# One decoder layer on one core: two more single matmuls in the stream, and the last 512 row columns in two banks

## The chip, the core and the metric

The kernel runs on one core of a Trainium2 chip. A core has TensorE (PE; loading its weights is shown apart, as PEld), VectorE (DVE), ScalarE (ACT), GpSimd (POOL) and SyncE (SP), which issues most of the transfers. TensorE reads from SBUF and writes to PSUM, whose banks hold 512 float32 numbers in each of 128 partitions. The metric is the device time of one execution in microseconds (us).

## The reference

One decoder layer on 256 prompt rows and 64 sample rows (8 × 8), all in float32, with shared weights:

```
xn = rms_norm(x, g_mix);  z = xn @ w_in            # B | C | h | q | k | v | gate_c | gate_a
y_conv = (B * conv3(C * h)) @ w_conv_out
y_attn = window_attention(q, k, v) @ w_attn_out     # window 128, bias, sinks
h = x + (sigmoid(gate_c) * y_conv + sigmoid(gate_a) * y_attn) @ w_o
hn = rms_norm(h, g_ffn)
h = h + (silu(hn @ w_gate) * (hn @ w_up)) @ w_down
y = rms_norm(h, g_final)
```

It returns y of the prompt and of the sample, the last keys and values, and the convolution states. The model width is 2048, the feed-forward width 5632.

## The kernel before

The 320 rows lie as columns: hT[p, k, t] holds feature 128 k + p of row t. Every weight tile is loaded once (`wraw`, on SP's queue) and split in two numbers of fewer bits, `whi` (ScalarE, line 129) and `wlo` (VectorE, line 130); the activations are split likewise (`xh`, `xl`). A product is then three matmuls of 320 columns for each 128 × 128 weights: hi by hi, hi by lo, lo by hi (`product`, line 176). All projections run so, one behind the other: k and v (`kv_product`), q, then four rounds of C, H and B, the gates, the outputs, the feed-forward layer.

Small work goes on beside them. The generator in `side_work` is advanced by one `yield` at each `tick`, that is behind each weight tile of a product. What it gives TensorE stands in the stream at that place. `first_norm` sums the squares over the partitions with two matmuls (`prb`, lines 199 and 200) and makes the row factors from it; `attention` makes the prompt's scores (`ps`, lines 549 and 552), the prompt's values (`prompt_pv`, `po`, line 611, matmuls of 64 and 32 rows or columns), and then the sample's attention (`pss`, line 716; `spo`, line 779). The PSUM tiles for it are handed out in turn from four banks (`ps_aux`).

`nudge` (line 195) is one matmul of 320 columns whose result nobody reads; its weights and columns are read as plain rows, not in the turned order of the products. There are three: in `kv_product`, behind the sample's scores, and behind the sample's values.

At the end the first 128 rows are wanted as rows. For columns 0 to 1535 that is done earlier. For the last 512 (from E0 = 1536), each k of the second half of w_down is a matmul with the activations as weights (`a_first(k)`, `a_low(k)`) and the 512 weight columns moving; they add up in one bank, `rowacc`, and the rest of h is added to it by four transposing matmuls with `ident` (line 1295). Then ScalarE squares the bank and sums it (`row_squares`, line 1162), a short chain on VectorE and ScalarE makes the factor r (lines 1309 to 1312), and the columns are scaled and sent (lines 1314 to 1325). Meanwhile VectorE scales the other 192 rows in seven pieces (line 1305), which SP sends.

Of the kernel before, what the change touches and what calls it, by code (L numbers as in the profile page):

```python
# [8 lines left out]
F32 = mybir.dt.float32  # L9
F32R = mybir.dt.float32r  # L10
AF = mybir.ActivationFunctionType
ALU = mybir.AluOpType
# [5 lines left out]
T = TP + NB * TS  # L18
# [9 lines left out]
P = 128  # L28
KC = D // P
# [9 lines left out]
E0 = D - 512  # L39
# [13 lines left out]
def hybrid_layer(ctx: ExitStack, tc: tile.TileContext, a: dict, o: list):  # L53
    nc = tc.nc
# [17 lines left out]
    def ps_aux(name):  # L72
        return aux[0].tile([P, 512], F32, tag="aux", name=name)
# [7 lines left out]
    def after(*marks):  # L81

        es = ExitStack()
        for m in marks:
            es.enter_context(tc.issue_after(m.ins))
        return es
# [56 lines left out]
    last = {}  # L143
# [49 lines left out]
    def nudge(rows, weights, n):  # L193
        x, w = (bass.AP(r.tensor, r.offset, [list(r.ap[0]), [1, m]]) for r, m in ((rows(0), n), (weights(0), P)))
        nc.tensor.matmul(ps_aux(u("nudge"))[:, :n], w, x, start=True, stop=True)
# [12 lines left out]
    ident = cst.tile([P, P], F32, name="ident")  # L208
# [50 lines left out]
    hT = xv[:, VW:VX].rearrange("p (k t) -> p k t", k=KC)  # L259
# [173 lines left out]
    def first_norm():  # L433

        squares(12, 13, 14, 15)
        nc.vector.tensor_scalar(nsink, sink_bc, -1.0, None, op0=ALU.mult)
        e_sb = pr.tile([P, 2, 2 * WIN], F32, tag="w", name="e_sb", bufs=1).rearrange("p g k -> p (g k)")[:NH, :EL]
        nc.vector.memset(e_sb, NEG)
        parts = two_rows(xacc, at_h(7), at_t[:, LEAD_A + 6 * at_row:LEAD_A + 6 * at_row + T])
        at, one_each = [_bucket(c) for c in range(WIN)], NBK // 2  # L440
        nc.gpsimd.tensor_copy(e_sb[:, WIN - 1:WIN - 1 + one_each], relT[:, :one_each])
        for b in range(one_each, NBK):
            c, n = WIN - 1 + at.index(b), at.count(b)
            nc.gpsimd.tensor_copy(e_sb[:, c:c + n], relT[:, b:b + 1].to_broadcast([NH, n]))
        yield
        prb = ps_aux("prb")
        over_partitions(prb[:, :T], parts)
        rstd_of(prb[:, :T], [P, T], "r1", spare, out=rb)
        nc.vector.tensor_scalar(rbq, rb, HD ** -0.5, None, op0=ALU.mult)
        for z in (vT, kT):  # L450
            for c in range(2):
                nc.vector.tensor_mul(z[:, c, :], z[:, c, :], rb)
        nc.vector.tensor_mul(rbsq, rb, rb)
        nc.gpsimd.dma_start(e_scr, e_sb)
        nc.gpsimd.dma_start(
            bias_s, bass.AP(e_scr.tensor, e_scr.offset + WIN - TS, [[EL, NH], [1, TS], [1, WIN + TS]])
        )
        for _ in range(3):
            yield

    yp = ExitStack()
    yy = yp.enter_context(tc.tile_pool(name="yy", bufs=1))
# [199 lines left out]
    def prompt_values(pv, scrs):  # L662
        sides = pv.tile([P, 2, WIN], F32, name="sides")
        nc.gpsimd.memset(sides, 1.0)
        nc.gpsimd.affine_select(
            out=sides[:, 0], in_=sides[:, 0], compare_op=ALU.is_ge, fill=0.0, base=-1, pattern=[[-1, WIN]],
            channel_multiplier=1,
        )
        nc.gpsimd.affine_select(
            out=sides[:, 0], in_=sides[:, 0], compare_op=ALU.is_ge, fill=0.0, base=B - 1, pattern=[[B, 4], [0, B]],  # L670
            channel_multiplier=-1,
        )
        nc.gpsimd.tensor_tensor(sides[:, 1], sides[:, 1], sides[:, 0], op=ALU.subtract)
        pts = [pv.tile([P, 2, 4, 4, B], F32, name=f"pT{kv}") for kv in range(NKV)]
        side = [pv.tile([P, 2, 2, 4, B], F32, name=f"side{kv}") for kv in range(NKV)]
        vm = [pv.tile([P, DKV], F32, name=f"vm{t}") for t in range(3)] + [vn[1]]
        mixes = ((0, 0, P, 0), (0, 0, B, 1), (1, 0, P, 0), (1, 0, 2 * B, 1), (2, 0, P, 1), (2, 3 * B, P, 0))
        for i in range(len(units) + 5):
            if i < len(units):
                kv, gp = units[i]  # L680
                nc.gpsimd.dma_start(pts[kv][:, gp].rearrange("p a n j -> p (a n j)"), scrs[i])
            if 2 <= i < 8:
                t, r0, r1, src = mixes[i - 2]
                nc.scalar.activation(vm[t][r0:r1], vn[src][r0:r1], AF.Copy)
            if i >= 5:
                kv, gp = units[i - 5]
                prompt_masked(sides, pts[kv][:, gp], side[kv][:, gp])
            yield
        prompt_pv(pts, side, vm)
        yield  # L690

    W2 = WIN + TS

# [417 lines left out]
    for half in range(2):  # L1111
# [41 lines left out]
        if half == 1:  # L1153
            ya = xp.tile([P, 2, D], F32, tag="xh", name="ya")
            y0, gfb = ya[:, 0, :], ya[:, 1, :]
            nc.gpsimd.dma_start(gfb, a["g_final"].partition_broadcast(P))
            ssf = op.tile([P, 4], F32, name="ssf")
            yacc = op.tile([P, TR], F32, name="yacc")

            def row_squares(i, src):  # L1160
                jk = op.tile([P, 512], F32, tag="jk", name=u("jk"))
                nc.scalar.activation(
                    jk[:, :src.shape[-1]], src, AF.Square, scale=D ** -0.5, accum_out=ssf[:, i:i + 1]
                )

            def rows_turn(c0):

                flipped = op.tile([P, 512], F32, tag="jk", name=u("yT")).rearrange("p (b k j) -> p b k j", b=4, k=4)
                nc.vector.transpose(
                    flipped.rearrange("p b k j -> p k b j"),  # L1170
                    hT[:, c0 // P:c0 // P + 4, 0:P].rearrange("p k (b i) -> p k b i", i=B),
                )
                rows = turned_rows(f"y_scr{c0}", flipped.rearrange("p b k j -> p (b k j)"), 4, 4 * B)
                nc.gpsimd.dma_start(y0[:, c0:c0 + 512], rows)

            def rows_of(c0):

                y = y0[:, c0:c0 + 512]
                nc.vector.tensor_add(y, y, ylow[:, c0:c0 + 512])
                row_squares(c0 // 512, y)  # L1180
                nc.vector.tensor_mul(y, y, gfb[:, c0:c0 + 512])

            def rest_square(k):
                sq = tmp("td", "sq")[:, :TR] if k else yacc
                nc.scalar.activation(sq, hT[:, k, P:T], AF.Square)
                return sq

            def rest_factor(k):
                rest = hT[:, k, P:T]
                last["hi"] = nc.scalar.activation(rest, rest, AF.Copy, scale=g_fin[:, k:k + 1])  # L1190

            def rest_of(chunks):

                for k in chunks:
                    sq = rest_square(k)
                    if k:
                        nc.vector.tensor_add(yacc, yacc, sq)
                    rest_factor(k)

            warm = op.tile([P, 1], F32, name="warm")  # L1200
            eps = op.tile([P, 1], F32, name="eps")
            nc.vector.memset(eps, EPS)
            with after(last["sig"]):
                nc.scalar.activation(warm, ones, AF.Abs_reciprocal_sqrt)
# [77 lines left out]
    for c in range(4):  # L1282
        rest_factor(E0 // P + c)

    for k in range(nf):
        (wh, wl), xhk, xlk = held[k], a_first(k), a_low(k)
        for m, x in enumerate((xhk, xlk)):
            last["mm"] = nc.tensor.matmul(rowacc, x, wh, start=k == m == 0, stop=k == nf - 1 and m == 1)
        if k == 3:
            with after(last["mm"]):  # L1290
                pn = ps_aux("pn")
                nc.tensor.matmul(pn[:, :TR], ones_r.bitcast(F32), yacc, start=True, stop=True)

                for c in range(4):
                    last["mm"] = nc.tensor.matmul(
                        rowacc[:, c * P:(c + 1) * P], hT[:, E0 // P + c, 0:P], ident, start=False, stop=False,
                        is_transpose=True,
                    )
    rf = sum_root(pn[:, :TR], [P, TR], "rn", op)
    yqs = [raw_tile().rearrange("p k n -> p (k n)")[:, :5 * TR].rearrange("p (k t) -> p k t", t=TR) for _ in range(4)]  # L1300
    ahead = ()
    for k0, k1 in ((0, 3), (3, 5), (5, 8), (8, 10), (10, 13), (13, 15), (15, KC)):
        yq = yqs[k0 // 5][:, k0 % 5:k0 % 5 + k1 - k0]
        with after(*ahead):
            ahead = (nc.vector.tensor_mul(yq, hT[:, k0:k1, P:T], rf.unsqueeze(1).to_broadcast([P, k1 - k0, TR])),)
        nc.sync.dma_start(y_r[:, k0:k1, :], yq)
    row_squares(3, rowacc)
    part = ssf[:, 3:4]
    nc.scalar.activation(r, part, AF.Abs_reciprocal_sqrt, bias=s3)
    nc.vector.scalar_tensor_tensor(v, part, -0.5, h3, op0=ALU.mult, op1=ALU.add)  # L1310
    nc.vector.scalar_tensor_tensor(v, r, r, v, op0=ALU.mult, op1=ALU.mult)
# [9 lines left out]
    act(1152, E0)  # L1321
    send(256, 768)
    nc.scalar.dma_start(y_0[:, 768:E0], y0[:, 768:E0])
    nc.vector.scalar_tensor_tensor(y0[:, es], rowacc, r, gfb[:, es], op0=ALU.mult, op1=ALU.mult)
    send(E0, D)


# [72 lines left out]
```

## Time and profile before

| | us |
|---|---|
| median of 3 runs | 1590.14 (1590.08 to 1590.64) |
| the profiled execution | 1589.86, of it the span from first to last instruction 1588.1 |
| TensorE busy | 1580.0 (99%) |
| VectorE, ScalarE, GpSimd busy | 881.6, 651.4, 128.5 |
| granted TensorE clock, mean | 0.999 |
| data moved | 266.09 MB, mean 168 GB/s |

In a row of the timeline stand the start, the duration, the engine, the line, the operation with output and inputs, the shapes and the count. Consecutive rows of one group are merged. Matmuls are pipelined, so their durations overlap; what one costs is the distance to the next start. In the view of groups, the numbers behind the bar are the time of the group in us, the mean of one in ns, and the idle time before them.

### The profile page before, as it was taken

The page shows a single profiled execution, that of the slowest core. Times are in us where ns is not written, and L with a number is a line of the kernel's source. Part 1 is how long each engine was busy: PE and PEld are TensorE (multiplying, and loading weights), DVE is VectorE, ACT ScalarE, POOL GpSimd, SP SyncE. Part 2 cuts the span into 40 slices and gives each one's busy share as a digit, 9 for nine tenths or more (in the row PEclk, how much of TensorE's full clock was granted, in tenths as well). Part 3 has the DMA queues.
Part 4 walks back from the last instruction along what each step waited for, and adds up shares of the span by engine and source line. Part 5 has one row for each costly group of instructions (what it writes and reads, how often), then busy time and mean ns, then how long its engine had stood idle before and what let it go on. Part 6 is the DMA issues. An engine that isn't in the chain of part 4 may idle for free.

```text
span 1588.1 us, 27217 instructions
## 1 busy us (share of the span) xinstructions
PE 1580.0 (99%) x11315; PEld 1566.3 (99%) x11315; DVE 881.6 (56%) x1263; ACT 651.4 (41%) x913; POOL 128.5 (8%) x228
## 2 busy tenths in 40 slices
PE   9999999999999999999999999999999999999998
PEld 9999999999999999999999999999999999999887
DVE  7888765544455445565555555553443455555556
ACT  7554444333333334344333333333333333344443
POOL 2223242000000003320000000000000000000000
PEclk9999999999999999999999999999999999999999
DMA  8666666454444544444444445455555544544653
GB/s 276 204 191 193 213 205 207 160 157 157 152 158 159 159 158 153 156 158 160 157 153 156 158 159 159 154 154 158 159 159 156 155 157 158 160 159 152 186 191 122
DMA packets 77714, 266.09 MB, mean 168 GB/s; under 512 B 9816, under 2 KB 13240, under 8 KB 77464
## 3 DMA queue, kind: packets, MB, share of 16 engines
q1 hardware_dynamic: 71880, 249.86, 49.7%
q0 software_dynamic: 5280, 13.82, 2.9%
q8 instruction: 88, 1.44, 0.4%
q10 hardware_dynamic: 432, 0.69, 0.1%
q14 instruction: 34, 0.28, 0.1%
HBM read 257.25 MB, written 9.04 MB: 168 GB/s over the span
## 4 chain that ended last, share of the span: by engine, by line
PE 99%; DVE 0%; ACT 0%; DVEq 0%; issue 0%
PE fu L176 19%; PE fg L176 19%; PE dn L1059 12%; PE wo L176 7%; PE ga L176 7%; PE gc L176 7%; PE B L176 3%; PE H L176 3%; PE C L176 3%; PE q L176 3%; PE ya L176 3%; PE yc L176 3%; PE dn L1084 3%; PE kv L372 2%; PE dn L1092 2%; PE dl L1088 1%
## 5 line engine op out<-in xcount | busy, mean ns | idle before, releaser
L130 DVE TENSOR_TENSOR wlo<-wraw,whi 128x1024 fp32r<-128x1024 f32 (+1 forms) x460 | 560.9, 1220 | 574.3 <-ACT whi L129 563.4
L129 ACT ACTIVATE whi<-wraw 128x1024 fp32r<-128x1024 f32 (+1 forms) x460 | 485.0, 1056 | 699.5 <-PE fu L176 131.5
L176 PE MATMUL fu<-hh_t,whi 128*128 128x320 f32 x704 | 205.0, 301 | 0.0
L176 PE MATMUL fu<-hl_t,whi 128*128 128x320 f32 x704 | 205.0, 301 | 0.0
L176 PE MATMUL fg<-hh_t,whi 128*128 128x320 f32 x704 | 205.0, 301 | 0.0
L176 PE MATMUL fg<-hl_t,whi 128*128 128x320 f32 x704 | 205.0, 301 | 0.0
L1059 PE MATMUL dn<-a_t,whi 128*128 128x320 f32 x896 | 162.6, 301 | 0.0
L176 PE MATMUL fg<-hh_t,wlo 128*128 128x320 f32 x704 | 158.8, 301 | 0.0
L176 PE MATMUL fu<-hh_t,wlo 128*128 128x320 f32 x704 | 158.8, 301 | 0.0
L1059 PEld LDWEIGHTS dn<-a_t,whi 128*128 128x128 f32 x896 | 137.5, 187 | 0.0
L176 PEld LDWEIGHTS fu<-hh_t,whi 128*128 128x128 f32 x704 | 131.7, 187 | 0.0
L176 PEld LDWEIGHTS fu<-hl_t,whi 128*128 128x128 f32 x704 | 131.6, 187 | 0.0
L176 PEld LDWEIGHTS fg<-hh_t,whi 128*128 128x128 f32 x704 | 131.6, 187 | 0.0
L176 PEld LDWEIGHTS fg<-hl_t,whi 128*128 128x128 f32 x704 | 131.6, 187 | 0.0
L176 PEld LDWEIGHTS fg<-hh_t,wlo 128*128 128x128 f32 x704 | 116.1, 187 | 0.0
L176 PEld LDWEIGHTS fu<-hh_t,wlo 128*128 128x128 f32 x704 | 116.1, 187 | 0.0
L1059 PE MATMUL dn<-a_t,wlo 128*128 128x320 f32 x448 | 103.9, 301 | 0.0
L1059 PEld LDWEIGHTS dn<-a_t,wlo 128*128 128x128 f32 x448 | 74.8, 187 | 0.0
L176 PE MATMUL gc<-xh_t,whi 128*128 128x320 f32 x256 | 74.5, 301 | 0.0
L176 PE MATMUL gc<-xl_t,whi 128*128 128x320 f32 x256 | 74.5, 301 | 0.0
L176 PE MATMUL ga<-xh_t,whi 128*128 128x320 f32 x256 | 74.5, 301 | 0.0
L176 PE MATMUL ga<-xl_t,whi 128*128 128x320 f32 x256 | 74.5, 301 | 0.0
(328 smaller groups left out, 2801.9 us busy)
## 6 DMA issues: line engine op xcount, KB each, us to landing
wraw<-in_w_in_dram SPq DMA_DIRECT2D x128, 512.0 KB, 3.7
wraw<-in_w_gate_dram SPq DMA_DIRECT2D x88, 512.0 KB, 3.6
wraw<-in_w_up_dram SPq DMA_DIRECT2D x88, 512.0 KB, 3.6
wraw<-in_w_down_dram SPq DMA_DIRECT2D x88, 512.0 KB, 3.6
wraw<-in_w_o_dram SPq DMA_DIRECT2D x32, 512.0 KB, 3.6
wraw<-in_w_conv_out_dram SPq DMA_DIRECT2D x16, 512.0 KB, 3.7
wraw<-in_w_attn_out_dram SPq DMA_DIRECT2D x16, 512.0 KB, 3.8
wraw<-in_w_kv_dram SPq DMA_DIRECT2D x6, 512.0 KB, 7.6
```

The costliest lines, as they stand in the source:

```text
L129: last["hi"] = nc.scalar.activation(hi, src, AF.Copy)
L130: last["lo"] = nc.vector.tensor_sub(lo, src, hi.bitcast(F32))
L176: last["mm"] = nc.tensor.matmul(turns(fives(ps[c][:, :T])), w[:, k, c * P:(c + 1) * P], turns(x(kc)), start=(kc == 0 and i == 0), stop=(kc ...
L372: last["mm"] = nc.tensor.matmul(turns(fives(ps[c][:, :T])), w[:, k, c * P:(c + 1) * P], turns(x(kc)), start=(kc == 0 and m == 0), stop=(kc ...
L1059: last["mm"] = nc.tensor.matmul(turns(fives(ps[c][:, :T])), parts[k][w][:, c * P:(c + 1) * P], turns(x(k)), start=k == 0 and m == 0, stop= ...
L1084: nc.tensor.matmul(turns(placed(ps[c])), parts[k][0][:, cs], turns(a_move(k)), start=k == 0, stop=False)
L1088: nc.tensor.matmul(low, a_low(k), parts[k][0], start=k == 0, stop=k == nf - 1)
L1092: last["mm"] = nc.tensor.matmul(turns(placed(ps[c])[:, :, 0:JT]), parts[k][1][:, cs], turns(a_move(k)[:, :, 0:JT]), start=False, stop=k == ...
```

## The change

It does three things. `first_norm` issues a nudge one step behind its two sums. `prompt_values` issues one a step behind `prompt_pv`. And the last 512 row columns are summed in two banks of 256 columns, `rowacc` and `rowacc2`: for all k but the last four, left and right in turn; for the last four, first all of the left, then all of the right. The left bank is squared by itself, its sum goes into s3 and h3 ahead of the last scaled piece of the other rows, and the last scaling is done half by half.

```
-        for _ in range(3):
-            yield
+        yield
+        nudge(xh, xl, T)
+        yield
+        yield
...
         prompt_pv(pts, side, vm)
         yield
+        nudge(xh, xl, T)
...
-    for k in range(nf):
+    halves = [rowacc, ps_aux("rowacc2")]
+    order = [(k, h) for k in range(nf - 4) for h in range(2)] + [(k, h) for h in range(2) for k in range(nf - 4, nf)]
+    for k, h in order:
         (wh, wl), xhk, xlk = held[k], a_first(k), a_low(k)
         for m, x in enumerate((xhk, xlk)):
-            last["mm"] = nc.tensor.matmul(rowacc, x, wh, start=k == m == 0, stop=k == nf - 1 and m == 1)
-        if k == 3:
+            last["mm"] = nc.tensor.matmul(
+                halves[h][:, :256], x, wh[:, h * 256:(h + 1) * 256], start=k == m == 0, stop=k == nf - 1 and m == 1
+            )
+        if (k, h) == (3, 1):
...
-                        rowacc[:, c * P:(c + 1) * P], hT[:, E0 // P + c, 0:P], ident, start=False, stop=False,
-                        is_transpose=True,
+                        halves[c // 2][:, c % 2 * P:(c % 2 + 1) * P], hT[:, E0 // P + c, 0:P], ident, start=False,
+                        stop=False, is_transpose=True,
...
+        if k1 == KC:
+            row_squares(3, halves[0][:, :256])
+            with after(*ahead):
+                nc.vector.tensor_add(s3, s3, ssf[:, 3:4])
+                ahead = (nc.vector.tensor_scalar(h3, s3, -0.5, None, op0=ALU.mult),)
...
-    row_squares(3, rowacc)
-    part = ssf[:, 3:4]
+    row_squares(4, halves[1][:, :256])
+    part = ssf[:, 4:5]
...
-    nc.vector.scalar_tensor_tensor(y0[:, es], rowacc, r, gfb[:, es], op0=ALU.mult, op1=ALU.mult)
+    for h in range(2):
+        cs = slice(E0 + h * 256, E0 + (h + 1) * 256)
+        nc.vector.scalar_tensor_tensor(y0[:, cs], halves[h][:, :256], r, gfb[:, cs], op0=ALU.mult, op1=ALU.mult)
```

Where the nudges land is set by the ticks. TensorE's order behind the first norm's sums, at the end of a weight tile of the first q product, before (`q` are the product's two banks, `whi` and `wlo` the weight parts; left out are two more of wlo):

```order
L176 MATMUL q_497<-xh_t,whi_614 128x16x5x4
L176 MATMUL q_497<-xl_t,whi_614 128x16x5x4
L176 MATMUL q_496<-xh_t,wlo_615 128x16x5x4
L176 MATMUL q_497<-xh_t,wlo_615 128x16x5x4
...
L176 MATMUL q_496<-xh_t,whi_644 128x16x5x4
L176 MATMUL q_496<-xl_t,whi_644 128x16x5x4
```

And with the change:

```order
L176 MATMUL q_497<-xh_t,whi_614 128x16x5x4
L176 MATMUL q_497<-xl_t,whi_614 128x16x5x4
L176 MATMUL q_496<-xh_t,wlo_615 128x16x5x4
L176 MATMUL q_497<-xh_t,wlo_615 128x16x5x4
...
L195 MATMUL nudge_642<-xh_t,xl_t 128x320
L176 MATMUL q_496<-xh_t,whi_646 128x16x5x4
```

The nudge stands between two weight tiles, 24 matmuls behind the sums; the rest of the order is as it was.

TensorE behind the prompt's values, where the last H product of a round ends and B begins, with the semaphores that are waited for, before and then with the change:

```order
L176 MATMUL H_2455<-xh_t,whi_2612 128x16x5x4
L176 MATMUL H_2455<-xl_t,whi_2612 128x16x5x4
L176 MATMUL H_2455<-xh_t,wlo_2613 128x16x5x4 x4
L176 MATMUL B_2676<-xh_t,whi_2680 128x16x5x4 [waits Activation_49]
L176 MATMUL B_2676<-xl_t,whi_2680 128x16x5x4
```

```order
L176 MATMUL H_2457<-xh_t,whi_2614 128x16x5x4
L176 MATMUL H_2457<-xl_t,whi_2614 128x16x5x4
L176 MATMUL H_2457<-xh_t,wlo_2615 128x16x5x4 x4
L195 MATMUL nudge_2642<-xh_t,xl_t 128x320 [waits DVE_49,PE_49]
L176 MATMUL B_2680<-xh_t,whi_2684 128x16x5x4 [waits Activation_49]
```

The nudge takes the first of the four banks of `po`, so it waits for VectorE, which empties them.

VectorE at the end, from the pieces of the other rows (`wraw` are their buffers) on, before and then with the change (`s` and `h` are s3 and h3, `vf` and `rr` the factor r, `ya` holds the rows):

```order
L1305 TENSOR_TENSOR wraw_16162<-xv,rnr 128x384
L1305 TENSOR_TENSOR wraw_16163<-xv,rnr 128x192
L1310 SCALAR_TENSOR_TENSOR vf<-ssf,h_16078 128x1
...
L1314 TENSOR_SCALAR ya<-ya,rr 128x512
L1324 SCALAR_TENSOR_TENSOR ya<-rowacc,rr,ya 128x512
```

```order
L1317 TENSOR_TENSOR wraw_16199<-xv,rnr 128x384
L1314 TENSOR_TENSOR s_16081<-s_16081,ssf 128x1
L1315 TENSOR_SCALAR h_16082<-s_16081 128x1
L1317 TENSOR_TENSOR wraw_16200<-xv,rnr 128x192
L1322 SCALAR_TENSOR_TENSOR vf<-ssf,h_16082 128x1
...
L1326 TENSOR_SCALAR ya<-ya,rr 128x512
L1338 SCALAR_TENSOR_TENSOR ya<-rowacc,rr,ya 128x256
L1338 SCALAR_TENSOR_TENSOR ya<-rowacc_16116,rr,ya 128x256
```

Two operations of one column now stand ahead of the last piece, and the last scaling is two operations.

More of the change, by code (lines that the diff above doesn't have):

```diff
@@ L1156, in hybrid_layer @@
             nc.gpsimd.dma_start(gfb, a["g_final"].partition_broadcast(P))
-            ssf = op.tile([P, 4], F32, name="ssf")
+            ssf = op.tile([P, 5], F32, name="ssf")
             yacc = op.tile([P, TR], F32, name="yacc")
```

## The prediction

> **What bounds the kernel now.** I read the page first, its busy times and the chain that ended last.
>
> ```profile
> span 1588.1 us, 27217 instructions
> PE 1580.0 (99%) x11315; PEld 1566.3 (99%) x11315; DVE 881.6 (56%) x1263; ACT 651.4 (41%) x913; POOL 128.5 (8%) x228
> PE 99%; DVE 0%; ACT 0%; DVEq 0%; issue 0%
> ```
>
> TensorE is the bound from end to end: 99% of the chain is matmuls. An inserted matmul therefore costs its place in the stream in full, nothing hides it, and whatever changes the pace of the stream counts once per matmul. The other engines matter only behind the last matmul. So I went to the timeline of TensorE, where the distance from start to start is what one matmul costs (the durations of 0.30 overlap). First an ordinary stretch, then the one behind the prompt's values, and the windows view of both:
>
> ```profile
> 230.30 0.30 PE L176 MATMUL C<-xl_t,whi 128*128 128x320 f32 x1
> ...
> 240.10 0.30 PE L176 MATMUL H<-xl_t,whi 128*128 128x320 f32 x1
> ```
>
> ```profile
> 204.12 0.30 PE L176 MATMUL B<-xh_t,whi 128*128 128x320 f32 x1
> ...
> 213.79 0.73 PE L176 MATMUL B<-xh_t,wlo 128*128 128x320 f32 x4
> ...
> 215.58 0.41 PE L176 MATMUL B<-xh_t,whi 128*128 128x320 f32 x1
> ...
> 219.09 0.31 PE L195 MATMUL nudge<-xh_t,xl_t 128*128 128x320 f32 x1
> 219.24 0.30 PE L176 MATMUL C<-xh_t,whi 128*128 128x320 f32 x1
> 219.38 0.30 PE L176 MATMUL C<-xl_t,whi 128*128 128x320 f32 x1
> ```
>
> ```profile
> 204.30:214.30 10.00, 10.00 (x72) 9.96 (x71) 6.50 (x9) 4.69 (x9) 9.59 (x21) 1.00 0.87 287
> 230.30:240.30 10.00, 10.00 (x74) 10.00 (x73) 4.33 (x5) 3.19 (x3) 4.04 (x8) 1.00 0.92 296
> ```
>
> In the ordinary stretch 70 matmuls start between the two rows: 9.80 / 70 = 0.1400 us each, and I find the same nearly everywhere. From 204.12 to 213.79 there are 68: 9.67 / 68 = 0.1422 each. The same shapes run 2.2 ns slower, at the same granted clock (1.00 in both windows) and without idle time. The slow pace begins behind the prompt's values (which end at 200.6), outlasts the sample's scores (214.45 to 215.58), and ends at the nudge of 219.09: from there it is 0.14 again. That is what a nudge does in this trace. It is worth 2.2 ns for each matmul up to the next thing that would have restored the pace anyway.
>
> **The nudge behind the first norm's sums** (one more matmul on TensorE, first row at 42.71 in the time of before). It costs what a nudge costs in an ordinary stretch, and saves what the stretch behind it loses now.
>
> ```profile
> 15.36 0.31 PE L195 MATMUL nudge<-xh_t,xl_t 128*128 128x320 f32 x1
> ...
> 16.52 0.30 PE L372 MATMUL kv<-xl_t,whi 128*128 128x320 f32 x1
> ```
>
> ```profile
> 39.06 0.30 PE L199 MATMUL prb<-at_t,ones_r 128*128 128x320 f32 x1
> 39.20 0.31 PE L200 MATMUL prb<-at_t,ones_r 128*128 128x320 f32 x1
> ...
> 39.77 0.30 PE L176 MATMUL q<-xl_t,whi 128*128 128x320 f32 x1
> ...
> 42.71 0.30 PE L176 MATMUL q<-xh_t,whi 128*128 128x320 f32 x1
> ```
>
> The nudge of 15.36 and seven ordinary matmuls took 1.16 us; seven take 0.98, so it cost 0.18 (its own 0.147 and some ns at each of the next few). Behind the norm's sums 21 matmuls start between 39.77 and 42.71: 2.94 / 21 = 0.140. The pace there is the good one already, so in this execution there is nothing to restore: **+0.18**. Lower end: not below −0.56, the rival below; upper end +0.18, unless the nudge harms the pace (another rival). No engine waits for it, and its bank is one that nobody has still to read.
>
> **The nudge behind the prompt's values**, ahead of the first B matmul, 204.12. By the row of 219.09 a nudge in a slow stretch costs 0.29 for itself and one matmul, 0.15 more than that matmul at 0.14. Behind it stand 72 slow matmuls up to the sample's scores (68 and the last four): 72 × 2.2 ns = 0.16 saved. If the scores do not bring the slow pace back, the 24 between 215.58 and 219.09 save 0.05 more. I take both: 0.15 − 0.21 = **−0.06**; ends −0.06 and, if nothing is cured, +0.18. This nudge also adds a wait, since its bank is the first of the four that the prompt's values filled. Who empties it:
>
> ```profile
> 201.09 2.74 DVE L643 TENSOR_TENSOR at_t<-po,at_t 128x256 fp32r<-128x256 f32 x8 [2.88 <-ACT at_t L642]
> ```
>
> The last of these eight ends at 203.83, 0.29 before TensorE comes to the nudge. Even if it waited for all eight it would not stand; and what is queued behind it, the B product, would be late by no more than the overrun.
>
> **The tail.** Before, the last 512 columns are 32 matmuls of 512 columns; now 64 of 256, with the weights loaded twice as often.
>
> ```profile
> 1572.47 2.02 PE L1288 MATMUL rowacc<-a_t 128*128 128x512 f32 x8
> 1574.32 0.53 PE L1292 MATMUL pn<-yacc,ones_r 128*128 128x192 f32 x2
> ...
> 1575.04 1.17 PE L1288 MATMUL rowacc<-a_t 128*128 128x512 f32 x4
> 1576.05 2.02 PE L1288 MATMUL rowacc<-more,a_t 128*128 128x512 f32 x8
> 1577.91 2.91 PE L1288 MATMUL rowacc<-whi,a_t 128*128 128x512 f32 x12
> ```
>
> ```profile
> 89.75 0.40 PE L549 MATMUL ps<-k,at_t 128*128 128x256 f32 x2
> ...
> 90.46 0.31 PE L176 MATMUL C<-xh_t,whi 128*128 128x320 f32 x1
> ```
>
> ```profile
> L1288 PE MATMUL rowacc<-whi,a_t 128*128 128x512 f32 x12 | 2.9, 391 | 0.0
> L549 PE MATMUL ps<-k,at_t 128*128 128x256 f32 x32 | 6.0, 279 | 0.0
> ```
>
> 512 columns cost (1577.91 − 1576.05) / 8 = 0.232. The nearest rows for 256 are the prompt's scores: six of 256 columns, each with its weights, from 89.75 to 90.46, 0.118. So the first 16 take 1.89 instead of 1.85, +0.04. The other 48 begin with the same pause behind the transposes (1576.05 − 1575.04 is 0.08 over 4 × 0.232); their last start is 1575.04 + 0.08 + 47 × 0.118 + 0.04 = 1580.71. Now the last ends at 1580.82 (row of 1577.91), and a 256 ends 0.279 behind its start: 1580.99, **+0.17**. A rule weighed here: the Trainium skill ("TensorE: Matmul & The Clock Gate", section "Back-to-back issue gap") gives N / 2.4 + 2.5 ns from matmul to matmul; that would be 109.2 ns for 256 columns and 215.8 for 512, a split of only +0.08 over 64 against 32, where the rows make +0.13; as an estimate by that page the tail would be 0.05 better. The rows of this trace lie above the rule in both sizes (118 and 232), so I go by the rows.
>
> Ends of this pitch: half of a 512, 0.116, and the 0.140 of a 320-column matmul, the next wider shape. That is −0.13 and +1.39 over 63 pitches; I take 0.118, the row of the same width.
>
> Behind the last matmul (the waits of ScalarE, VectorE and the last sends):
>
> ```profile
> 1580.86 0.60 ACT L1162 ACTIVATE jk<-rowacc 128x512 f32<-128x512 f32 x1 [5.24 <-PE rowacc L1288]
> 1581.35 0.19 ACT L1162 ACTIVATION_READ_ACCUMULATOR jk<-rowacc 128x1 f32 x1
> ...
> 1582.36 0.75 DVE L1314 TENSOR_SCALAR ya<-ya,rr 128x256 f32<-128x256 f32 x2
> 1582.74 1.39 SPq L1316 DMA_DIRECT2D out_dram<-ya  x3
> 1583.02 0.75 DVE L1324 SCALAR_TENSOR_TENSOR ya<-rowacc,rr,ya 128x512 f32<-128x512 f32 x1
> ```
>
> ```profile
> L1185 ACT ACTIVATE sq<-xv 128x192 f32<-128x192 f32 x15 | 5.3, 359 | 12.3 <-DVE xv L1270 5.5 <-DVE yacc L1197 3.6 <-DVE xv L1105 3.2
> ...
> L1181 DVE TENSOR_TENSOR ya<-ya 128x512 f32<-128x512 f32 x3 | 2.1, 691 | 1.3 <-ACT jk L1162 1.3
> ```
>
> ```profile
> L851 DVE TENSOR_TENSOR qt<-q,rbq 128x256 f32<-128x256 f32 x8 | 3.4, 420 | 0.1
> ```
>
> ```profile
> 1580.69 0.36 DVE L1305 TENSOR_TENSOR wraw<-xv,rnr 128x192 f32<-128x192 f32 x1
> ```
>
> The left half's squares now run while TensorE makes the right half: eight matmuls, 8 × 0.118 = 0.94, cover one ACTIVATE and its read of the sum. What stays on the path is a Square of 256 instead of 512. Between 192 columns (359 ns) and 512 (0.60) a column costs 0.75 ns, so **−0.19**. The added sum and h3 on VectorE (two operations of one column, about 0.16 each) stand ahead of the last quotient of the other rows. The left sum is there at 1580.99 − 0.94 + 0.04 + 0.41 + 0.19 = about 1580.7, when that quotient started until now (1580.69); it and its send go about 0.35 later, and the send is not among the last, which begin at 1582.74: 0. The last scaling becomes two of 256. VectorE does 256 in 420 ns and 512 in 691, so a half costs about 0.75 − 0.27 = 0.48, and with the overlap of the pair at 1582.36 two take 0.87: **+0.12**. That is not covered, since the last send waits for the right part. Tail: 0.17 − 0.19 + 0.12 = **+0.10**, ends −0.15 (the low pitch, the scaling's extra covered by the transfers ahead of it) and +1.5 (the high pitch).
>
> **The sum** is 0.18 − 0.06 + 0.10 = +0.22. The profiled execution took 1589.86 (span 1588.1 and 1.8 around it) and would take 1590.1; the median of the runs, 1590.14, lies 0.28 above it, and on it I forecast 1590.3 to 1590.4. A change of under 0.2% (3.2 us) is about what a measurement here cannot tell from none; this one is a fifteenth of that.
>
> **Rivals.** (a) *A slow stretch that the profiled execution did not have.* The median is 0.28 over it, and the slow pace is there in one stretch, so the norm's sums may leave it in other executions. Up to the first prompt's scores (89.75) 336 matmuls × 2.2 ns = 0.74; the first nudge would gain 0.56 instead of losing 0.18. Against it: the only trace shows 0.140 there. Time 1589.6. (b) *The small matmuls do not reach 0.118 in the tail*, since their weights change at every instruction and come from tiles that are read as rows: at 0.140 the tail is +1.5 and the time 1591.7. For it: 512 columns cost 0.232 here. (c) *The change harms the pace, the other side.* The pace is a state that a few odd matmuls set and that nothing ordinary clears. If the new nudge of 42.71 leaves the slow one, it lasts to the prompt's values, 1104 matmuls, 2.4 us: 1592.7, still inside 0.2%. If the shifted sequence leaves it slow behind the last nudge at 254.9, the 8600 matmuls up to 1460 lose 18.9 us: 1609. It decides from about 1450 slow matmuls (3.2 us) on. Against it: the three nudges of before all end in 0.140. (d) *The change does nothing for the pace:* the second nudge leaves 0.1422; +0.18 instead of −0.06, 1590.6, inside the main range.
>
> **How the numbers follow.** Main case, (d) included, 0.76, time 1590.3, its own range 1589.9 to 1591.0 (the runs of before already spread from 1590.08 to 1590.64). (a) 0.10, (b) 0.07, (c) 0.04 for the short and 0.015 for the long form; 0.015 for what I do not see, split over both signs. A range from 1589.5 to 1591.2 holds the main case and (a), 0.86 less some noise. Faster by over 0.2% would need 1450 matmuls that run slow now, and I find 96: 0.01. Slower by over 0.2%: the long form of (c) and half of the unseen, 0.025. The rest, 0.965, is no change.
>
> **What would show it.** A nudge at about 42.7 with 0.18 lost around it; a nudge at 204.3, and 0.140 instead of 0.1422 behind it up to the sample's scores; 64 matmuls in the tail at 0.118, the left Square about 0.9 ahead of the right one, a right Square of about 0.41. I would be wrong if a long stretch reads 0.142, if TensorE shows a gap at the second nudge, or if the tail's pitch is near 0.14.

## The result, and the profile after

The changed kernel took 1602.43 us (median of 22 runs, 1590.03 to 1603.39), the kernel before 1590.24 in 22 runs beside them (1589.63 to 1603.14). The ratio is 1.0061, with a 95% interval of 1.0047 to 1.0075: slower by 0.6%, where I had forecast no change (the ratio takes in the runs of both groups named below; the two medians lie 12.2 us apart, 0.8%). A single execution of either kernel falls near 1590 or near 1602, with nothing between. Of the changed kernel's runs 19 of 22 were near 1602, of the runs before 3 of 22. The profiled executions were one of each majority: 1602.66 after, 1589.86 before.

The page of the changed kernel, its span, its busy times and the shares of the chain that ended last:

```profile
span 1601.0 us, 27294 instructions
PE 1592.9 (99%) x11349; PEld 1580.8 (99%) x11349; DVE 883.1 (55%) x1266; ACT 652.0 (41%) x915; POOL 128.2 (8%) x228
PE 99%; DVE 0%; ACT 0%; issue 0%; DVEq 0%
```

TensorE is still the bound, and 34 more matmuls cannot be 12.9 us. So the pace had changed somewhere, and the windows view finds where. Its columns are the stretch, its length, then busy time and instructions of PE, PEld, DVE, ACT and POOL, the granted clock, the DMA share and GB/s. First before, then after:

```profile
206.00:213.00 7.00, 7.00 (x51) 7.00 (x51) 5.23 (x7) 2.70 (x4) 6.99 (x12) 1.00 0.90 277
256.00:700.00 444.00, 444.00 (x3174) 444.00 (x3173) 227.13 (x269) 173.41 (x202) 35.60 (x34) 1.00 0.50 159
720.00:1400.00 680.00, 680.00 (x4860) 680.00 (x4859) 335.74 (x410) 250.12 (x295) 0.00 (x0) 1.00 0.51 157
```

```profile
206.00:213.00 7.00, 7.00 (x52) 7.00 (x51) 4.88 (x7) 3.31 (x5) 6.99 (x13) 1.00 0.94 304
256.00:700.00 444.00, 444.00 (x3173) 444.00 (x3172) 226.57 (x269) 174.44 (x205) 36.47 (x36) 1.00 0.49 159
720.00:1400.00 680.00, 680.00 (x4783) 680.00 (x4783) 331.19 (x402) 246.57 (x287) 0.00 (x0) 1.00 0.49 155
```

From 256 to 700 the two are alike. From 720 to 1400 TensorE is busy without a gap in both, at a granted clock of 1.00 in both, but does 4783 matmuls instead of 4860: 142.2 ns each against 139.9 (those cut at the edges counted). Where that begins is in the timeline of TensorE, after:

```profile
705.32 0.73 PE L176 MATMUL fg<-hh_t,wlo 128*128 128x320 f32 x4
705.89 0.31 PE L199 MATMUL pss<-a_t,ones_r 128*128 128x320 f32 x1
706.03 0.31 PE L200 MATMUL pss<-a_t,ones_r 128*128 128x320 f32 x1
706.18 0.30 PE L176 MATMUL fu<-hh_t,whi 128*128 128x320 f32 x1
...
707.17 0.30 PE L176 MATMUL fu<-hl_t,whi 128*128 128x320 f32 x1
```

Here stand the sums of the *second* norm (`pss`, lines 199 and 200: the same helper as for the first norm), which the change does not touch. The seven matmuls from 706.18 to 707.17 take 0.99, about 0.142 each. The same place before, six matmuls from 705.58 to 706.42 in 0.84, 0.140 each:

```profile
705.29 0.30 PE L199 MATMUL pss<-a_t,ones_r 128*128 128x320 f32 x1
705.43 0.31 PE L200 MATMUL pss<-a_t,ones_r 128*128 128x320 f32 x1
705.58 0.30 PE L176 MATMUL fu<-hh_t,whi 128*128 128x320 f32 x1
...
706.42 0.30 PE L176 MATMUL fu<-hh_t,whi 128*128 128x320 f32 x1
```

The pace stays so. Behind these sums stand 5472 product matmuls up to the second half of w_down; they take 778.24 us after (706.18 to 1484.42) and 766.08 before (705.58 to 1471.66), 142.22 and 140.00 ns each. That is 12.2 of the 12.9 us. About 0.4 more is lost at the start, where it varies from execution to execution: there the first products step by 267 ns, up to 6.46 us instead of 5.66, and the profile's record of the granted clock begins at 6.56 instead of 5.74. Over the profiles of before, after and the experiments this record begins anywhere from 3.5 to 6.6. So the first nudge stands at 43.15, where its place was forecast from 42.71. About 0.3 is the sum of the three local terms.

**Two streams of 140 ns.** Why do the same sums leave 140.00 before and 142.22 after, when what runs into them has a pace of 140 in both? The groups by line, from 300 to 690, in both kernels (mean ns of one behind the comma), before and then after:

```profile
L176 PE MATMUL gc<-xh_t,whi 128*128 128x320 f32 x224 | 65.2, 301 | 0.0
```

```profile
L176 PE MATMUL gc<-xh_t,whi 128*128 128x320 f32 x224 | 65.3, 302 | 0.0
```

A matmul lasts 301 ns before and 302 after, and not as a mean alone: shortest, median and longest of the 224 are all 301, or all 302. The step, from start to start, is 140 in both, so the span does not show it. The ends of matmuls are modelled in these profiles, so I take the 1 ns as a mark that tells two streams apart, and not as work. The weight loads of these `gc` rows carry it too: 187 ns shortest, median and longest before, 187, 188 and 188 after. I call them kind 301 and kind 302. Both kinds occur in the kernel before itself, which has this row from 222 to 245, behind its second nudge:

```profile
L176 PE MATMUL H<-xh_t,whi 128*128 128x320 f32 x31 | 9.1, 302 | 0.0
```

After, the same stretch has the other kind:

```profile
L176 PE MATMUL H<-xh_t,whi 128*128 128x320 f32 x28 | 8.2, 301 | 0.0
```

With that the chain can be followed, stretch by stretch (odd I call a matmul that belongs to no ordinary product: the nudges, the sums, the attention's). Before: the prompt's values leave the slow pace (durations of 303 to 305), the sample's scores keep it, the nudge of 219.09 turns it into kind 302, the sample's values turn kind 302 into 301, the last nudge, 254.88, and the second norm's sums leave 301 as it is. After, the timeline of TensorE:

```profile
204.73 0.31 PE L195 MATMUL nudge<-xh_t,xl_t 128*128 128x320 f32 x1
204.88 0.30 PE L176 MATMUL B<-xh_t,whi 128*128 128x320 f32 x1
205.02 0.30 PE L176 MATMUL B<-xl_t,whi 128*128 128x320 f32 x1
...
219.66 0.31 PE L195 MATMUL nudge<-xh_t,xl_t 128*128 128x320 f32 x1
...
252.37 0.30 PE L176 MATMUL B<-xh_t,whi 128*128 128x320 f32 x1
...
254.93 0.73 PE L176 MATMUL B<-xh_t,wlo 128*128 128x320 f32 x4
255.50 0.31 PE L195 MATMUL nudge<-xh_t,xl_t 128*128 128x320 f32 x1
255.64 0.30 PE L176 MATMUL B<-xh_t,whi 128*128 128x320 f32 x1
```

The new nudge at 204.73 turns the slow pace into kind 301; the scores and the nudge of 219.66 leave 301. The sample's values turn 301 into the slow pace: from 252.37 to 254.93 there are 18 matmuls, 2.56 / 18 = 0.1422. The last nudge turns this into kind 302, and the second norm's sums turn 302 into the slow pace, which nothing ends up to 1484. So the sample's values and the last nudge together exchange the kinds, and the new nudge makes another one arrive. In all 13 profiled executions of kernels that read in turns (before, after and the experiments) the same holds: 301 ahead of the values goes with the slow pace behind them (eight profiles, seven of them with the new nudge), 302 with 140 (five, none with it). In e11 the records scatter by 1 ns; there 301 is the median.

### The profile page after: what moved, and what is told of

The parts are those of the page before. It is cut to its first block, busy times and chain, and to the rows that moved or that the text cites. A ratio compares the mean times of both kernels' runs of the same rounds, so it can differ in the third digit from the quotient of the medians.

```text
span 1601.0 us, 27294 instructions
## 1 busy us (share of the span) xinstructions
PE 1592.9 (99%) x11349; PEld 1580.8 (99%) x11349; DVE 883.1 (55%) x1266; ACT 652.0 (41%) x915; POOL 128.2 (8%) x228
## 4 chain that ended last, share of the span: by engine, by line
PE 99%; DVE 0%; ACT 0%; issue 0%; DVEq 0%
PE fu L176 19%; PE fg L176 19%; PE dn L1062 12%; PE wo L176 7%; PE gc L176 7%; PE ga L176 7%; PE B L176 3%; PE H L176 3%; PE q L176 3%; PE C L176 3%; PE ya L176 3%; PE yc L176 3%; PE dn L1087 3%; PE kv L372 2%; PE dn L1095 2%; PE dl L1091 1%
```

## The experiments

The expectations name the theories they tell apart. The first that I held is theory A: what the second norm's sums leave depends on whether the last nudge ahead of them met a slow or a fast stream. e4 overturned that, and the two kinds were read from the profiles afterwards.

**The three parts alone** (e1 to e3, one of the three things each).

> The kernel before with the nudge behind the first norm's sums alone. The second norm's sums leave the slow pace (0.1423 us a matmul) in the changed kernel, some 12.3 us to the end. Theory A (what the sums leave depends on the kind of stream that the last nudge met: a slow one makes the next odd matmuls slow, a fast one does not): this nudge meets a fast stream, and the prompt's values leave the slow pace behind it either way, so nothing later changes: 1590.4 in most executions, as before plus 0.18. Theory B (any shift in time of the sums against other work decides): shifted by 0.18, so 1602 can come, or a mix. Theory C (the tail or the wider ssf, through where things lie): 1590.4.

> The kernel before with the nudge behind the prompt's values alone. Theory A: it makes the sample's scores meet a fast stream, so the next nudge meets a fast one, the sample's values turn slow, the last nudge meets a slow one, and the second norm's sums turn slow: 1602.4 in most executions, with the same three stretches as the changed kernel. Theory B: a mix, with no such order. Theory C: 1590.2.

> The kernel before with the tail in two banks alone, no new nudge. Theory A and B: nothing ahead of the second norm's sums differs, so as before, 1590.1 to 1590.4 in most executions, with the tail's own effect of 0 to 0.2 us. Theory C: 1602.4.

e1 took 1590.36 (median; 1 of 6 runs near 1602; ratio 0.9985, 0.9945 to 1.0025). e3 took 1590.39 (2 of 6 near 1602; 0.9997, 0.9955 to 1.004). e2 took 1602.24, all 6 near 1602 (1.0047, 1.0013 to 1.0082; four of the eleven runs of before beside them were near 1602 too). The windows view of e1, e2 and e3:

```profile
720.00:1400.00 680.00, 680.00 (x4860) 680.00 (x4859) 335.88 (x411) 250.53 (x296) 0.00 (x0) 1.00 0.50 157
```

```profile
720.00:1400.00 680.00, 680.00 (x4783) 680.00 (x4782) 331.33 (x401) 245.98 (x286) 0.00 (x0) 1.00 0.49 155
```

```profile
720.00:1400.00 680.00, 680.00 (x4859) 680.00 (x4858) 335.87 (x410) 250.34 (x295) 0.00 (x0) 1.00 0.50 157
```

The nudge behind the prompt's values alone makes the slow stretch, with the same steps as in the whole change. The other two parts by themselves show no loss.

**A nudge in the middle of the long stretch** (e4).

```diff
+        if mp == 3:
+            nudge(xh, xl, T)
         ps = product(
             lambda k0, n: load_cols(w_co, k0, n, c0), 8,
```

> The changed kernel with one more nudge, behind a gate product of the fourth round (near 400 us), where the stream is fast. Theory A: the last nudge ahead of the second norm's sums now meets a fast stream, as in the kernel before, so the sums leave the fast pace: 1590.6 in most executions, 12 us less than the changed kernel for one more matmul. Theory B: shifted by 0.18, no reason for one or the other, a mix. Theory C: 1602.6.

It took 1602.90, all 6 runs near 1602 (1.0052, 1.0017 to 1.0086). The windows view and the timeline:

```profile
720.00:1400.00 680.00, 680.00 (x4784) 680.00 (x4783) 331.38 (x402) 246.60 (x288) 0.00 (x0) 1.00 0.49 155
```

```profile
410.81 0.31 PE L195 MATMUL nudge<-xh_t,xl_t 128*128 128x320 f32 x1
410.95 0.30 PE L176 MATMUL yc<-cv_h,whi 128*128 128x320 f32 x1
411.10 0.30 PE L176 MATMUL yc<-cv_l,whi 128*128 128x320 f32 x1
```

Theory A fell here: this nudge meets a fast stream and leaves it kind 302 (302 in the rows of `gc` ahead of it and behind), and the sums turn it slow all the same. That is what made me read durations beside steps.

**A nudge behind the second norm's sums** (e5 on the changed kernel, e6 on the one before), which ends the slow pace whichever way it came.

```diff
         psu = product(...)
+        if half == 0 and fpair == 0:
+            nudge(hh, hl, T)
```

> The changed kernel with one more nudge behind the first up product, 192 matmuls behind the second norm's sums. If the whole loss is the slow pace that the sums leave, and a nudge ends it there as it does at 219 and 255: the slow stretch is 192 matmuls (0.44 us) and the rest runs at 0.1400, so 1590.9 in every execution, and no execution at 1602. If the slow pace of the rest has another cause (the layout, the transfers of that stage), or comes back by itself: 1602.6.

> The kernel before with that one nudge alone. Seven of its 33 executions so far were near 1602.5. If those are the same slow pace behind the second norm's sums: no execution near 1602 any more, 1590.3 to 1590.9 (0.18 for the nudge, 0.44 where the sums left the slow pace). If they are something else: still one in five near 1602.

e5 took 1590.56 (1590.11 to 1591.08, 11 runs; 0.9996, 0.9982 to 1.001), e6 1590.34 (1589.7 to 1590.69, 11 runs; 1.0000, 0.9992 to 1.0009). No run of either came near 1602. The windows view and the timeline of e5:

```profile
707.00:717.00 10.00, 10.00 (x73) 10.00 (x72) 9.07 (x14) 5.91 (x8) 0.00 (x0) 1.00 0.47 155
720.00:1400.00 680.00, 680.00 (x4859) 680.00 (x4858) 335.84 (x410) 250.40 (x295) 0.00 (x0) 1.00 0.50 157
```

```profile
718.51 0.73 PE L176 MATMUL fu<-hh_t,wlo 128*128 128x320 f32 x4
719.07 0.31 PE L195 MATMUL nudge<-hh_t,hl_t 128*128 128x320 f32 x1
719.22 0.30 PE L176 MATMUL fg<-hh_t,whi 128*128 128x320 f32 x1
```

In e5 the sums do leave 142.2, and one matmul 13 us later ends it for the rest. (The slow stretch is 96 matmuls, not the 192 of the expectation, so it costs 0.21 us and not 0.44.) That shows that the loss is this stretch and nothing else: with all three parts in place and the stretch cured, e5 stands 0.35 over the 1590.21 of the 23 runs of before beside it. The profiled execution of e6 went another way than the profile before: the sample's scores turned the slow pace into kind 301, from there all went as in the changed kernel, and the new nudge ended the slow stretch behind the sums. So the kernel before has both ways too, and this one would have ended near 1602 without the nudge; none of its runs near 1602 was profiled.

**How the columns are read** (e7, e8). Every ordinary product reads its 320 columns through `turns`, four-column groups in turn from five pieces of 64; the second matmul of the sums and the nudges read them in a row. e7 makes the sums' second matmul read in turns (its low part lies in one piece, without the gaps that the high part has); in e8 `turns` changes nothing, so that all products read, and write to PSUM, piece by piece in a row.

```diff
 # e7
-        nc.tensor.matmul(out, ones_r, lo, start=False, stop=True)
+        nc.tensor.matmul(turns(fives(out)), ones_r, turns(fives(lo)), start=False, stop=True)
 # e8
-        return ap.rearrange("p s (i b) -> p i s b", b=4)
+        return ap
```

> The changed kernel with the second matmul of both norms' sums read and written in the turned order of the products (the same numbers, only another order of the columns). Theory: an odd order of reading is what moves the pace. Then the sums are like any product matmul, the stream that comes in at 0.1400 goes out at 0.1400: 1590.4 in every execution. Rival: what moves it is where the sums' columns or weights lie, or the wait at that place: still 1602.4 in most.

> The changed kernel with all products reading their columns in the plain order of the five pieces instead of the turned one (same numbers, same count). If the two paces are two ways in which the turned reads can fall against the weight reads: one pace throughout, whatever the nudges do, either near 0.140 (1590) or worse than the slow one (above 1602). If the pace has nothing to do with the order of reading: the same two paces at the same places, 1602.

e7 took 1602.56 (5 of 6 near 1602; 1.0065, 1.0044 to 1.0087): the sums, reached by kind 302, turn it slow as before, so the order of that one read does not do it by itself. e8 took 1661.96 (one run). Its windows view:

```profile
300.00:400.00 100.00, 100.00 (x684) 100.00 (x684) 48.73 (x59) 37.08 (x44) 0.00 (x0) 1.00 0.46 151
800.00:900.00 100.00, 100.00 (x684) 100.00 (x683) 49.86 (x62) 37.14 (x43) 0.00 (x0) 1.00 0.47 150
```

It has one pace ahead of the second norm's sums and behind them, and no nudge changes it: 3216 matmuls from 265.64 to 737.32, 146.7 each. So the paces of 140.0 and 142.2 belong to the turned order, and both are better than the plain one (reading and writing were not changed apart).

**Other sums** (e9 on the changed kernel, e10 on the one before). Both parts of the second norm's sums are put in ordinary rows, and both matmuls read in turns, as a product does.

```diff
-over_partitions(pss[:, :T], two_rows(hacc, a_hi(FH[0] - 1), a_spare))
+hi, lo = a_hi(FH[0] - 1), a_lo(FH[0] - 1)
+nc.scalar.activation(hi, fives(hacc), AF.Copy)
+nc.vector.tensor_sub(lo, fives(hacc), hi.bitcast(F32))
+for part in (hi, lo):
+    nc.tensor.matmul(turns(fives(pss[:, :T])), ones_r, turns(part), start=part is hi, stop=part is lo)
```

> The changed kernel with the second norm's two sums read exactly as a product reads: both parts of the squares lie in rows of the second matrix (five pieces with the 16 spare numbers between them) and both matmuls take the turned order. What is left that is odd is the weights, ones. (In the run before this one the low part was turned but lay in one piece, so it was still an odd read.) Theory D: an odd read of the moving columns moves the pace. Then 1590.4 in every execution, 0.1400 on both sides of the sums. Rival E: the weights' place (the tile of ones is read ahead, under the last gate matmul, whose step already grew to 0.144) does it: still 1602.4 in most.

> The kernel before with the same two sums. Theory D: 1590.2 in every execution, none near 1602, the best version so far, without a further nudge. Rival E: about one in six near 1602, as before.

e9 took 1590.46 (10 of 12 near 1590; 0.9945, 0.9923 to 0.9966), e10 1590.35 (9 of 12 near 1590; 0.9952, 0.9928 to 0.9977). The ratios are below 1 because 21 of the 23 runs of before beside them were near 1602. The profiled execution of e9 had kind 302 ahead of the sums, that of e10 kind 301; their windows view:

```profile
720.00:1400.00 680.00, 680.00 (x4860) 680.00 (x4859) 335.76 (x410) 250.40 (x296) 0.00 (x0) 1.00 0.50 157
```

```profile
720.00:1400.00 680.00, 680.00 (x4784) 680.00 (x4783) 331.14 (x401) 246.05 (x287) 0.00 (x0) 1.00 0.49 155
```

Neither of the theories written for these two held. Such sums don't always hand on a good pace, and don't always hand on what they meet: in these two profiles they turn kind 301 slow and kind 302 into 301, at 140, the reverse of the old ones. The counts agree: where most runs of before were near 1602, most of e10 are near 1590. So how the sums are laid out and read decides which kind they turn. The layout of the low part, its place and the order changed together here, and which of them does it is not shown.

**Without the last nudge** (e11, on the changed kernel).

```diff
     two_to(*parts, flipped)
-    nudge(xh, xl, T)
```

> The changed kernel without the last of the old nudges (255, behind the sample's values). Theory A2 (a nudge that meets a slow stream leaves a second kind of 0.1400, and this kind is what the second norm's sums turn slow): without it the stream stays at 0.1422 from the sample's values to the sums, 3200 matmuls, 7.1 us; what the sums make of a slow stream is not known: 1597.4 if they leave 0.1400, 1609.7 if they leave 0.1422. Rival (the last nudge is of no weight, the pace behind it would come back by itself): 1602.3.

It took 1597.31 (one run). Its windows view:

```profile
256.00:700.00 444.00, 444.00 (x3124) 444.00 (x3123) 223.35 (x265) 172.03 (x201) 33.89 (x35) 1.00 0.49 158
720.00:1400.00 680.00, 680.00 (x4859) 680.00 (x4859) 338.59 (x417) 253.38 (x300) 0.00 (x0) 1.00 0.51 157
```

The slow pace that the sample's values leave now lasts to the second norm's sums, 3240 matmuls, 7.1 us, and these meet a slow stream and leave a good one, which the expectation had left open. So the last nudge is what turned the slow pace into the kind 302 that the sums make slow.

**The version to keep** (e12): the kernel before and one nudge behind the first weight tile, 24 matmuls, of the product that follows the second norm's sums.

```diff
+tiles_in = []
+def behind_sums():
+    tiles_in.append(0)
+    if len(tiles_in) == 2:
+        nudge(hh, hl, T)
 ...
-    hh, hl, "fu",
+    hh, hl, "fu", loaded=behind_sums if half == 0 and fpair == 0 else None,
```

> The kernel before with one nudge behind the first weight tile of the up product that follows the second norm's sums, 24 matmuls behind the sums; no other edit. Theory: whichever kind of 0.1400 comes in, and whether or not the sums turn it slow, the nudge leaves a fast stream to the end. 1590.2 to 1590.7 in every execution, none near 1602, on any chip; the kernel before on the same chip has some or many near 1602. Rival (the nudge cures only one of the two kinds, or the pace must have settled for longer): some executions near 1602.

It took 1590.39 (1589.97 to 1591.09, 11 runs; 1.0001, 0.9992 to 1.001), beside 15 runs of before of which none came near 1602 (1589.86 to 1591.39), against the expectation of some or many. So it wins nothing over the kernel before there, costs nothing measurable, and its gain was not put to the test: in its profile kind 301 reached the sums, which left 140 before the nudge. That a nudge 24 matmuls behind the sums would end the slow pace is argued from the nudges of 204.73 and 255.50, which did so 24 matmuls behind the values. Over all comparisons the kernel before came near 1602 in 29 of 94 runs (3 of 22, 4 of 11, 1 of 23, 21 of 23, 0 of 15). The three kernels with a nudge behind the second norm's sums did in 0 of 33; but beside e5 and e6 before did in 1 of 23, and beside e12 in none. What the counts show is e5: 0 of 11, where the changed kernel without that nudge had 19 of 22 in the first comparison, and e7, run beside e5, 5 of 6.

## Why the prediction was wrong

**The first nudge, forecast +0.18, was right.** The timeline after:

```profile
43.15 0.31 PE L195 MATMUL nudge<-xh_t,xl_t 128*128 128x320 f32 x1
43.29 0.31 PE L176 MATMUL q<-xh_t,whi 128*128 128x320 f32 x1
...
44.30 0.30 PE L176 MATMUL q<-xl_t,whi 128*128 128x320 f32 x1
```

The nudge and seven matmuls take 1.15 to 1.16, against 0.98 for seven: 0.17 to 0.18 lost, and 140 on both sides of it. Rival (a), a slow stretch there, did not show.

**The second nudge, forecast −0.06 for its own stretch, was right too.** By the rows shown with the result, the nudge and one matmul take 0.29 (204.73 to 205.02); it did not wait, and behind it the pace is 140: 52 matmuls from 206 to 213 where before there were 51. The sample's scores then kept 140, as I had taken them to; in e4, e7 and e11 they did not, so that part held by luck. Rival (d) is out.

**The tail, forecast +0.10, came to +0.14.** The timeline after:

```profile
1585.23 2.07 PE L1293 MATMUL rowacc<-a_t 128*128 128x256 f32 x16
...
1588.84 2.06 PE L1293 MATMUL rowacc<-more,a_t 128*128 128x256 f32 x16
1590.74 3.02 PE L1293 MATMUL rowacc<-whi,a_t 128*128 128x256 f32 x24
1592.84 0.39 ACT L1165 ACTIVATE jk<-rowacc 128x256 f32<-128x256 f32 x1 [4.45 <-PE rowacc L1293]
...
1593.86 0.38 ACT L1165 ACTIVATE jk<-rowacc 128x256 f32<-128x256 f32 x1 [0.54 <-PE rowacc L1293]
1595.14 0.75 DVE L1326 TENSOR_SCALAR ya<-ya,rr 128x256 f32<-128x256 f32 x2
1595.81 0.87 DVE L1338 SCALAR_TENSOR_TENSOR ya<-rowacc,rr,ya 128x256 f32<-128x256 f32 x2
```

The pitch of 256 columns is (1590.74 − 1588.84) / 16 = 0.119, as taken from the prompt's scores (0.118); the formula of the Trainium skill that I weighed ("TensorE: Matmul & The Clock Gate", section "Back-to-back issue gap"), 109.2 ns, does not agree with it; the section gives it for an isolated matmul and says itself that it misses a stream with weight loads. From the start of `rowacc` to the right Square it is 8.63 (1585.23 to 1593.86) where it was 8.39: +0.24 against +0.17. From there to the first scaling 1.28 against 1.50: −0.22 against −0.19. The two scalings take 0.87, as forecast: +0.12. The left Square stands 1.02 ahead of the right one (forecast 0.94), which lasts 0.38 (0.41). Rival (b) is out.

**What failed is the price of rival (c), its long form**, which had 0.015, while in the sum the pace behind the last nudge stood at nothing. Its mechanism was named, and its place was nearly right: I set it behind the last nudge, and it came at the second norm's sums, 12.2 us instead of 18.9. The step that was wrong is the argument against it, "the three nudges of before all end in 0.140". It treated 0.140 as one state, and it stopped at the last nudge instead of going on to the last odd matmul. Two readings of the profile before would have raised that chance. First, the second norm's sums at 705.29 go through the same helper as the first norm's, and more matmuls stand behind them than behind any other odd matmul in that kernel; my list of steps never came to them, because the diff does not touch them. Second, the durations of 302 from 222 to 245 and of 301 from 300 on, at the same step, already said that there are two streams of 140, and that one of them reached the sample's values and the other left them. With one trace of one way through the chain, the sign could not have been derived; 0.965 for no change was too much for a change that inserts such a matmul ahead of two others. The three runs of before, all near 1590, also hid that the kernel has a second result.

**What stays open.** What the two kinds are in the chip, 1 ns apart in the records and equal in step, no run here tells; nor why the sample's scores go one way or the other on the same stream: with the new nudge ahead they left 301 in the profiles of after, e2, e5 and e9 and turned it slow in those of e4, e7 and e11, and without it they kept the slow pace in five profiles and ended it in one (e6). The kinds are not the whole state either: where the nudge near 219 meets a slow stream, it leaves 302 in the five profiles without the new nudge and 301 in e4, e7 and e11, though the slow records look alike. And not odd matmuls alone change the pace: in the profile of e10 four early products, at 32.18 to 32.71, start 0.21, 0.14 and 0.18 apart, kind 302 at 140 stands ahead of them and 142.2 behind, up to the first norm's sums. With the new nudge both ways led to 301 behind the nudge of 219.66, and so to 1602; what the few runs of the changed kernel near 1590 did differently was never in a profile. The share of runs near 1602 of the kernel before went from 0 of 15 to 21 of 23; the four comparisons of the experiments were made at other times and each on another chip, which are not told apart. That the scores' way sets the share is argued from e6, not shown.

## What to carry to other kernels

In a kernel that is one stream of matmuls, price an inserted matmul also by what it hands on: follow the pace past the edit to the longest stretch that nothing resets, even where the diff does not reach. Put the resetting matmul behind the last odd matmul ahead of that stretch: 96 matmuls behind it, in e5 and e6, it ended the slow pace, and cost nothing measurable. Before a sum of tenths is trusted, look at the spread of many executions: one profile shows one way through.

## What the runs showed of the hardware

At a granted clock of 1.00 and without a gap, the same 320-column matmul runs at 140.0 or at 142.2 ns, and either pace is kept over 5472 matmuls (before and after); read and written in a row instead of in turns it runs at one pace, 146.7 ns (e8). The formula of the Trainium skill ("TensorE: Matmul & The Clock Gate", section "Back-to-back issue gap"), N / 2.4 + 2.5 for an isolated matmul, gives 135.8 for 320 columns; none of the three agrees with it.

Two streams of the same step can differ in the recorded duration of each matmul, 301 or 302 ns, uniformly over hundreds of instructions in twelve of the thirteen profiles, and an odd matmul turns one of them slow and not the other: the second norm's sums as they were turn kind 302, laid out and read as in e10 they turn kind 301.
